# Merge inputs loaded tile by tile with the mLSTM product first, and an attention iteration of four positions, in a fused encoder layer on one core

## The chip, the cores and the metric

The kernel runs on one core of a Trainium2 chip. The metric is the device time of one execution in microseconds (us), and three executions of each kernel are given as a median with the lowest and the highest. The engines are named as in the profile: PE is TensorE (matrix products; PEld its weight loads), DVE is VectorE, ACT is ScalarE, POOL is GpSimd, and SP is the engine from whose queue nearly all DMAs are issued.

## The reference

One encoder layer over two sequences, a prompt of 1024 tokens and a sample of 2048 tokens, of width 1024, each with 16 learned meta tokens put in front. Cut to what matters here:

```python
xn = rmsnorm(h, g_pre)
proj = xn @ w_in + b_in                          # 1024 -> 6672 columns
na_q, na_k, na_v, na_z, ml_qk, ml_v, ml_z, ml_o, ml_g, mg = split(proj)
ya = (neighbourhood_attention(na_q, na_k, na_v, na_rpb) * silu(na_z)) @ w_a    # 512 -> 1024
yb = (mlstm(conv(ml_qk), ml_v, ml_g, ml_o, head_g)   * silu(ml_z)) @ w_b       # 512 -> 1024
ga, gb = split(sigmoid(mg))
y  = (ga * ya + gb * yb) @ w_out                 # the merge, 1024 -> 1024
out = h + rmsnorm(y, g_post)                     # meta tokens dropped
```

The attention has 8 heads of 64 and sees windows of 8 grid rows by 16 columns with a relative bias `na_rpb`. The mLSTM has 4 heads of 128 and runs in both directions. All products are carried to nearly float32 precision.

## The kernel before, in words

**Products.** Every float32 operand is split into a high part in the PE's format (an ACT copy, `AF.Copy`) and the remainder (a DVE subtraction), and a product is three matmuls: high by high, high by low, low by high (`mm3`, lines 144 to 146).

**Two streams on PE.** The order of PE's instructions is written out by the program; the other engines' orders come from the compiler's scheduler. Two Python generators make the order. `dense` yields, after each handful of matmuls, what they cost PE: mostly `6 * C512` (six matmuls of 512 columns, 1.41 us) or `12 * C256` (1.44 us). `sparse` runs the mLSTM and the attention, whose steps depend on ACT and DVE, and yields after each step how much dense work should follow it. `run` adds up what `sparse` yields, and draws dense pieces until that is used up; when `dense` yields `True` it cannot go on, and `sparse` continues alone.

**The dense stream** follows `PLAN`: the input projection in groups of columns (`m` for the mLSTM, `n` for the attention, `g` for the merge gates) for sequence 0 (the prompt) and for the two halves of sequence 1 (the sample), and merges `("f", s, b)`, one for each 512 tokens. The plan is m and n of sequence 0, m of both halves of sequence 1, n of its second half, g of sequence 0, merges (0,0) and (0,1), then n and g of what is left, and merges (1,0) to (1,3), which are the end of the kernel.

**The sparse stream** follows `STEPS`: mLSTM of sequence 0, attention of sequence 0 (row tiles 0 and 1), mLSTM of sequence 1, attention of sequence 1 (row tiles 0 to 3). An mLSTM starts with its gates (`ml_gates`: a load of `g_t`, then `yield 3.0`, then small steps, the first PE step being line 754 and the next line 762), goes on with states and outputs, and ends with a normalisation (`ml_norm`, whose transposes are line 1205).

**The attention** (`na`) takes a row tile of 512 tokens, a pair of heads (`pr`, 0 to 3), a head (`hh`) and a column block (`cb`, 0 to 3): 64 units for sequence 0 and 128 for sequence 1. An iteration has three positions, each ended by `yield A_NA` with `A_NA` = 1.52: the scores of unit u (lines 665 and 666), then the scaling of u and the turning of u-1 (transposes, line 690), then the output product of u-2 (line 702). The steps of `na_prep`, which load and split the inputs of the next head, are spread over the positions. Ahead of the first unit the prep runs with `5 + 5 * 1` yields of `A_NA`. After the last column block of a head pair, line 710 multiplies by the gate and line 711 stores the pair's tile to `YA`; when `pr` is 3 the row tile is entered in `self.done`.

**The merge** (`final`) of a tile needs eight tiles of 128 by 512: four of `YA[s][b]` (k = 0 to 3, attention, one for each pair of heads) and four of `YB[s]` (k = 4 to 7, mLSTM). `yload` loads them into `yr` tiles (the ring `st` of 4 buffers, shared with the projection's stores and the residual loads `xres`) and splits them (lines 1248 and 1249). It returns at once unless all eight are done (`ready`). Otherwise it is spread beside the work before the merge, as a hook in the second half of the previous merge or as the side of a projection group; if it was not, `final` runs all of it at its start. The first half of a merge, called F1 here, goes over eight feature tiles `ft`: for `br` = 0 (attention) and then 1 (mLSTM) a product over four k into a PSUM bank, a gated multiply (line 1284, whose gate tiles `tg` are loaded two feature tiles ahead into the ring `stT`), and after the second the sum and its split `mh`, `mlo`. Beside F1 runs `final_out` of the previous merge: residual loads `xres`, line 1377, stores. The second half, F2, is `w_out`: lines 1305 to 1307, with `yo` out of it. Weights come through `whi` and `wlo`, rings of 4 buffers, 512 KB for each load, in the order of use, on SP like all else. SP issues in order: a DMA that waits holds those behind it.

Of the kernel before, what the change touches and what calls it, by code (L numbers as in the profile page):

```python
# [17 lines left out]
P = 128  # L18
# [86 lines left out]

NBW = 4
C512, C256 = 0.235, 0.12
A_NA, A_D, A_A, A_N, A_G = 1.52, 1.63, 1.63, 1.85, 1.3


class K:
# [384 lines left out]
    def spread(self, gen, chunks, until=None):  # L496

        steps = 22 if until is None else 12

        def side(last=False):  # L500
            nonlocal acc, over
            acc += steps / chunks
            while not over and (acc >= 1.0 or last):
                acc -= 1.0
                x = next(gen, "end")
                over = x == "end" or (until is not None and x == until)
        acc, over = 0.0, False
        return side

    def group(self, s, t0, meta, cols, reuse, nxt):  # L510

        todo = [(s, t0, meta), (s, t0 + 512, False)]
        jobs = self.layout(cols)
        nb = None
        for j, (kind, c) in enumerate(jobs):
            if kind == "tm":
                yield from self.tm_unit(c[0], [(x,) + h for x, h in zip(self.xs, todo)], c[1])
                continue
            ws = self.wtake(len(c))
            last = j == len(jobs) - 1  # L520
            for hf in range(2):
                side = None
                if j == 0 and hf == 0 and not reuse:
                    side = self.spread(self.build_half(*todo[1], self.xs), 15)
                elif last and nxt and nxt[0] == "f":
                    side = self.spread(self.yload(*nxt[1:]), 15) if hf else None
                elif last and nxt:
                    if hf == 0:
                        nres = []
                        nb = self.build_half(*nxt, nres)  # L530
                        side = self.spread(nb, 15, "scaled")
                    else:
                        side = self.spread(nb, 15)
                for col, w in zip(c, ws):
                    for cost in self.fm_half(col, w, self.xs[hf], *todo[hf], done=self.wdone if hf else None):
                        yield cost
                        if side:
                            side()
# [13 lines left out]
    def na(self, s, rts):  # L552

        tc, nc, i = self.tc, self.nc, self.i
        rows = _row_types(SEQLEN[s] // 64)
        with tc.tile_pool(name=f"na{s}{rts[0]}", bufs=1, side="right", reuse_waits="tile") as np_:
            self.qB = [np_.tile([P, 4, P], F32R, name=f"qB{j}") for j in range(2)]
            self.kx = [np_.tile([P, 16, 64], F32R, name=f"kx{j}") for j in range(2)]
            self.gts = [np_.tile([P, 17, 48], F32, name=f"gt{j}") for j in range(2)]
            for q in self.qB:  # L560
                nc.gpsimd.dma_start(q[64:128], i["onehot"].rearrange("a (b c) -> a b c", b=4))
            for g in self.gts:
                nc.gpsimd.memset(g[:, 0, :], 0.0)
                nc.gpsimd.memset(g[:, 16, :], 0.0)
            heads = [(rt, pr, hh) for rt in rts for pr in range(4) for hh in range(2)]
            n = len(heads)
            prep = self.na_prep(np_, s, rows, heads, 0)
            for k in range(6):
                next(prep, None)
                for _ in range(1 if k else 5):  # L570
                    yield A_NA
            self.na_bias(rows, heads, 0)
            cur, nxt = self.head, None
            units = [(j, cb) for j in range(n) for cb in range(4)]
            ready = {}
            for u in range(len(units) + 2):
                if u < len(units):
                    j, cb = units[u]
                    if cb == 0:
                        cur = self.head  # L580
                        prep = self.na_prep(np_, s, rows, heads, j + 1) if j + 1 < n else iter(())
                        next(prep, None)
                    ready[u] = [cur, heads[j], cb, None, None, self.gts[j % 2]]
                    self.na_scores(np_, ready[u], rows)
                    if j + 1 < n and cb == 0:
                        self.na_bias(rows, heads, j + 1)
                yield A_NA
                if u < len(units):
                    self.na_scale(np_, ready[u])
                    if cb:  # L590
                        next(prep, None)
                if 1 <= u <= len(units):
                    self.na_turn(np_, ready[u - 1], rows)
                yield A_NA
                if u >= 2:
                    self.na_out(np_, ready.pop(u - 2), s)
                if u < len(units) and cb >= 2:
                    next(prep, None)
                yield A_NA

    def na_bias(self, rows, heads, j):
# [94 lines left out]
    def na_out(self, np_, unit, s):  # L696
# [12 lines left out]
        if hh and cb == 3:  # L709
            nc.vector.tensor_tensor(yg, yg, zt, op=ALU.mult)  # L710
            nc.sync.dma_start(self.YA[s][rt][pr][:, :], yg)
            if pr == 3:
                self.done.add(("na", s, rt))


    def ml_gates(self, s, keep, mp, res):
# [9 lines left out]
            nc.gpsimd.memset(gt[:, 0, 8 * d + 4:8 * d + 8], 1.0e4)  # L726
        nc.sync.dma_start(gt[:NM, 0, :], self.GA[s][0:NM, :])
        nc.sync.dma_start(gt[:, 1:, :], self.GA[s][NM:, :].rearrange("(c p) g -> p c g", p=P))
        yield 3.0
        gv = gt.rearrange("p c (d k h) -> p d k c h", d=2, k=2)  # L730
        lf = t("g_lf", [P, 2, NC_, 4])
        e = t("g_e", [P, 2, NC_, 4])
# [495 lines left out]
        self.done.add(("ml", s))  # L1228


    def ready(self, s, b):
        return {("ml", s), ("na", s, b)} <= self.done

    def yload(self, s, b):

        if not self.ready(s, b):
            return
        nc, fp, n = self.nc, self.wp, 512
        yh = fp.tile([P, KT, n], F32R, name="yh", tag="xh", bufs=2)
        yl = fp.tile([P, KT, n], F32R, name="yl", tag="xl", bufs=2)  # L1240
        self.y = (s, b), yh, yl
        yr = {}
        for k in range(KT + 2):
            if k < KT:
                yr[k] = fp.tile([P, n], F32, name="yr", tag="st", bufs=4)
                nc.sync.dma_start(yr[k], self.YA[s][b][k][:, :] if k < 4 else self.YB[s][k - 4][:, b * n:(b + 1) * n])
            if k >= 2:
                nc.scalar.activation(yh[:, k - 2], yr[k - 2], AF.Copy)  # L1248
                nc.vector.tensor_tensor(yl[:, k - 2], yr.pop(k - 2), yh[:, k - 2].bitcast(F32), op=ALU.subtract)  # L1249
                yield  # L1250

    def final(self, s, b, nxt):
        nc, fp, i = self.nc, self.wp, self.i
        n, t0 = 512, 512 * b
        if self.y is None or self.y[0] != (s, b):
            for _ in self.yload(s, b):
                pass
        _, yh, yl = self.y
        mh = fp.tile([P, KT, n], F32R, name="mh", tag="xh", bufs=2)
        ml = fp.tile([P, KT, n], F32R, name="mlo", tag="xl", bufs=2)  # L1260
# [2 lines left out]
        def gates(ft):  # L1263
            if ft < KT:
                tgs[ft] = []
                for br in range(2):
                    tg = fp.tile([P, n], F32, name="tg", tag="stT", bufs=4)
                    nc.sync.dma_start(tg, self.GT[s][8 * br + ft][:, t0:t0 + n])
                    tgs[ft].append(tg)

        gates(0)
        gates(1)
        for ft in range(KT):
            w = self.wtake(1)[0]
            ms = tgs.pop(ft)
            for br in range(2):
# [5 lines left out]
                if br:  # L1282
                    self.wdone()
                nc.vector.scalar_tensor_tensor(ms[br], ms[br], 1.0, p, op0=ALU.add, op1=ALU.mult)
                if br:
# [23 lines left out]
        for cq in range(4):  # L1309
# [7 lines left out]
            for tt in range(4):  # L1317
# [19 lines left out]
                if nxt and hook is None:  # L1337
                    if nxt[0] != "f":
                        nres = []
                        hook = self.build_half(*nxt, nres)  # L1340
                    elif self.ready(*nxt[1:]):
                        hook = self.yload(*nxt[1:])
                if hook:
                    next(hook, None)
                yield (3 if tt in first else 12) * C256
        if hook:
            for _ in hook:
                pass
        if nxt:
            self.fout = self.final_out(s, t0, yt, ssq, 0, 4)  # L1350
            if nxt[0] != "f":
# [31 lines left out]
    def dense(self, ctx):  # L1383
# [19 lines left out]
        for j, (s, t0, cols) in enumerate(PLAN):  # L1403
            nxt = PLAN[j + 1] if j + 1 < len(PLAN) else None
            if s == "f":
                if post is None:
                    post = self.gpost = self.gain("g_post")
                while not self.ready(t0, cols):
                    yield True
                yield from self.final(t0, cols, nxt and (nxt if nxt[0] == "f" else nxt[:2] + (False,)))  # L1410
                continue
            same = [0 <= k < len(PLAN) and PLAN[k][:2] == (s, t0) for k in (j - 1, j + 1)]
# [81 lines left out]
```

## Time and profile before

| | |
|---|---|
| time, three runs | 2925.31 us median (2923.33 to 2926.53) |
| the profiled execution | 2927.06 us, its span 2925.1 us |
| PE busy | 2824.3 us, 97% |
| DVE, ACT busy | 1745.3 us (60%), 1287.4 us (44%) |
| granted PE clock, mean over the span | 0.986 |
| DMA | 675.26 MB, mean 231 GB/s |

The span is what the profiler's records cover; the time of the execution is 1.96 us longer. A busy PE is not a PE at its peak, since the profile models the ends of matmuls, so the distance between the starts of matmuls is read beside it. Idle time of an engine other than PE costs nothing by itself.

### The profile page before, as it was taken

To read this page: it belongs to the slowest core of one execution; us is meant where nothing else is said; L and a number is where in the kernel's file an instruction comes from. 1 tells how busy PE (TensorE), PEld (TensorE's weight loads), DVE (VectorE), ACT (ScalarE), POOL (GpSimd) and SP (SyncE) were. 2 spreads that over 40 slices of the span, in tenths; PEclk is the share of its full clock that TensorE was granted. 3 is DMA by queue.
4 is the path that set the end of the run, shared out by engine and by line. 5 is a ranking of instruction groups with operands and counts; after the bars stand their busy time and mean duration, and the time that the engine had idled before them with its cause. 6 is when DMAs were issued, how large, how long until landed. Compare 5 with 4: busy or idle time off the path is not lost.

```text
span 2925.1 us, 49552 instructions
## 1 busy us (share of the span) xinstructions
PE 2824.3 (97%) x17488; PEld 2514.2 (86%) x17488; DVE 1745.3 (60%) x4722; ACT 1287.4 (44%) x3114; POOL 23.0 (1%) x107
## 2 busy tenths in 40 slices
PE   6999999999799999899999999999999999999998
PEld 6998898899689988798887998888888888979877
DVE  5233566556556765466558786565555557786843
ACT  4112546443344444356566554523444445544421
POOL 1000000000000000000000000000000000000000
PEclk9999999999899999999999999999999999999999
DMA  9655566755775654469669898578569659797875
GB/s 348 222 174 184 194 224 235 251 180 195 254 248 155 200 167 142 138 219 312 212 213 356 279 346 281 154 261 273 178 190 298 192 163 289 249 303 242 274 245 194
DMA packets 438760, 675.26 MB, mean 231 GB/s; under 512 B 52240, under 2 KB 253024, under 8 KB 438512
## 3 DMA queue, kind: packets, MB, share of 16 engines
q1 hardware_dynamic: 437392, 669.41, 70.0%
q0 software_dynamic: 1120, 2.69, 0.4%
q8 instruction: 138, 2.26, 0.3%
q14 instruction: 110, 0.90, 0.1%
HBM read 455.05 MB, written 216.90 MB: 230 GB/s over the span
## 4 chain that ended last, share of the span: by engine, by line
PE 82%; DMA 9%; DVE 5%; ACT 1%; SPq 1%; issue 1%; ACTq 0%; DVEq 0%
PE pj L144 14%; PE pj L145 14%; PE pj L146 14%; PE pj L412 6%; PE pj L413 6%; PE pj L414 6%; PE pj L1305 3%; PE pj L1307 3%; PE pj L1306 3%; PE sm L702 3%; PE tr L690 3%; DMA tg<-gt 1%; PE sc L665 1%; PE sc L666 1%; PE sm L146 1%; DMA um<-ud 1%
## 5 line engine op out<-in xcount | busy, mean ns | idle before, releaser
L144 PE MATMUL pj<-xh,whi 128*128 128x512 f32 (+1 forms) x1824 | 722.3, 396 | 1.0 <-DVE xl L310 1.0
L145 PE MATMUL pj<-xl,whi 128*128 128x512 f32 (+1 forms) x1824 | 702.3, 385 | 0.1
L146 PE MATMUL pj<-xh,wlo 128*128 128x512 f32 (+1 forms) x1824 | 700.5, 384 | 0.0
L412 PE MATMUL pj<-whi,xh 128*128 128x256 f32 (+3 forms) x1576 | 451.0, 286 | 0.0
L413 PE MATMUL pj<-wlo,xh 128*128 128x256 f32 (+3 forms) x1576 | 444.6, 282 | 0.0
L414 PE MATMUL pj<-whi,xl 128*128 128x256 f32 (+3 forms) x1576 | 444.1, 282 | 0.0
L146 PEld LDWEIGHTS pj<-xh,wlo 128*128 128x128 f32 x1824 | 345.5, 189 | 72.3
L144 PEld LDWEIGHTS pj<-xh,whi 128*128 128x128 f32 x1824 | 346.0, 190 | 55.9 <-DVE xl L310 1.2
L145 PEld LDWEIGHTS pj<-xl,whi 128*128 128x128 f32 x1824 | 346.5, 190 | 53.2 <-DVE xl L310 0.4
L412 PEld LDWEIGHTS pj<-whi,xh 128*128 128x128 f32 (+1 forms) x1576 | 294.3, 187 | 1.2
L413 PEld LDWEIGHTS pj<-wlo,xh 128*128 128x128 f32 (+1 forms) x1576 | 294.0, 187 | 1.0
L414 PEld LDWEIGHTS pj<-whi,xl 128*128 128x128 f32 (+1 forms) x1576 | 293.9, 187 | 0.9
L673 ACT ACTIVATE prb<-sc,mx 128x384 f32<-128x384 f32 (+2 forms) x192 | 120.1, 625 | 237.4 <-DVE mx L669 236.3
L1305 PE MATMUL pj<-whi,mh 128*128 128x256 f32 x768 | 221.7, 289 | 2.7 <-DVE yo L1333 2.7
L1307 PE MATMUL pj<-whi,mlo 128*128 128x256 f32 x768 | 217.7, 283 | 0.0
L1306 PE MATMUL pj<-wlo,mh 128*128 128x256 f32 x768 | 217.4, 283 | 0.0
L669 DVE CUSTOM_DVE_ANT_1 sc<-sc,gt 128x384 f32<-128x384 f32 (+2 forms) x192 | 118.9, 619 | 96.3 <-PE sc L666 86.8
L708 DVE TENSOR_TENSOR yg<-sm,yg 64x128 f32<-64x128 f32 x384 | 108.4, 282 | 108.0 <-ACT yg L706 100.2
L421 DVE TENSOR_TENSOR stT<-pj,bb 128x256 f32<-128x256 f32 (+3 forms) x197 | 83.2, 422 | 143.8 <-PE pj L414 142.7
L144 PE MATMUL pj<-yh,whi 128*128 128x512 f32 x384 | 158.3, 412 | 8.5 <-ACT yh L1248 6.1
L693 DVE TENSOR_TENSOR pts<-tr,pts 96x512 fp32r<-96x512 f32 (+2 forms) x192 | 131.6, 685 | 47.8 <-ACT pts L692 46.0
L145 PE MATMUL pj<-yl,whi 128*128 128x512 f32 x384 | 153.9, 401 | 0.2 <-DVE yl L1249 0.2
(234 smaller groups left out, 5074.6 us busy)
## 6 DMA issues: line engine op xcount, KB each, us to landing
whi<-wh SPq DMA_DIRECT2D x176, 512.0 KB
wlo<-wl SPq DMA_DIRECT2D x176, 512.0 KB
wh<-whi SPq DMA_DIRECT2D x64, 512.0 KB
wl<-wlo SPq DMA_DIRECT2D x64, 512.0 KB
wraw<-w_in SPq DMA_DIRECT2D x48, 512.0 KB
gt<-st SPq DMA_DIRECT2D x96, 256.0 KB
tg<-gt SPq DMA_DIRECT2D x96, 256.0 KB
xh<-xh SPq DMA_DIRECT2D x6, 2048.0 KB
```

Of the source, the lines that this page charges most:

```text
L144: mm(out, ah, bh, start=start, stop=False)
L145: mm(out, ah, bl, start=False, stop=False)
L146: mm(out, al, bh, start=False, stop=stop)
L412: nc.tensor.matmul(o, xh, wh, start=k == 0, stop=False)
L413: nc.tensor.matmul(o, xh, wl, start=False, stop=False)
L414: nc.tensor.matmul(o, xl, wh, start=False, stop=k == KT - 1)
L669: nc.vector.tensor_tensor_reduce(out=so, in0=so, in1=gt[:, g0:g0 + ns, c0:c0 + 32], op0=ALU.add, op1=ALU.min, scale=-1.0, scalar=3.0e38, a ...
L673: nc.scalar.activation(pr_[:, :N].rearrange("p (b a c) -> p b a c", b=4, c=8), sc[:, :N].rearrange("p (a b c) -> p b a c", b=4, c=8), AF.E ...
L693: nc.vector.tensor_tensor(pts[:ks, :, 1, :], pt[:ks], pts[:ks, :, 0, :].bitcast(F32), op=ALU.subtract)
L1305: nc.tensor.matmul(o, mh[:, k, xs], wh, start=k == 0, stop=False)
L1306: nc.tensor.matmul(o, mh[:, k, xs], wl, start=False, stop=False)
L1307: nc.tensor.matmul(o, ml[:, k, xs], wh, start=False, stop=k == KT - 1)
```

## The change

Three things are changed.

1. **Merge inputs.** The attention's stores are entered in `self.done` for each pair, `("na", s, b, pr)`, instead of for the row tile. `yload` takes the mLSTM's tiles first, then the attention's pairs; where a tile is not yet done it splits what it holds and yields `"wait"`, on which the loops beside it leave off. It is started always (`ystart`), also when its inputs are not all done. `final` does the mLSTM product (`br` = 1) ahead of the attention product (`br` = 0), and takes each tile when its product needs it; where that is not to be had it yields `True`, in place of the loop ahead of the merge that waited for `ready`.
2. **Attention iteration.** Four positions with `A_NA` = 1.12 instead of three with 1.52: scores of u; scaling of u; turning of u-1; output of u-2. The prep ahead of the first unit has `6 + 5 * 2` yields.
3. **mLSTM gates.** The yield after the load of `g_t` is 6.0 instead of 3.0.

The core of the diff:

```diff
-A_NA, A_D, A_A, A_N, A_G = 1.52, 1.63, 1.63, 1.85, 1.3
+A_NA, A_D, A_A, A_N, A_G = 1.12, 1.63, 1.63, 1.85, 1.3
...
-                for _ in range(1 if k else 5):
+                for _ in range(2 if k else 6):
                     yield A_NA
...
                     self.na_scale(np_, ready[u])
                     if cb:
                         next(prep, None)
+                yield A_NA
                 if 1 <= u <= len(units):
                     self.na_turn(np_, ready[u - 1], rows)
+                    if u < len(units) and cb >= 2:
+                        next(prep, None)
                 yield A_NA
                 if u >= 2:
                     self.na_out(np_, ready.pop(u - 2), s)
-                if u < len(units) and cb >= 2:
-                    next(prep, None)
                 yield A_NA
...
             nc.sync.dma_start(self.YA[s][rt][pr][:, :], yg)
-            if pr == 3:
-                self.done.add(("na", s, rt))
+            self.done.add(("na", s, rt, pr))
...
-        yield 3.0
+        yield 6.0
...
     def yload(self, s, b):
-        if not self.ready(s, b):
-            return
...
+        for k in (4, 5, 6, 7, 0, 1, 2, 3):
+            need = ("ml", s) if k > 3 else ("na", s, b, k)
+            if need not in self.done:
+                while todo:
+                    split()
+                    yield
+                while need not in self.done:
+                    yield "wait"
+            yr = fp.tile([P, n], F32, name="yr", tag="st", bufs=4)
+            nc.sync.dma_start(yr, self.YA[s][b][k][:, :] if k < 4 else self.YB[s][k - 4][:, b * n:(b + 1) * n])
+            todo.append((k, yr))
+            if len(todo) == 3:
+                split()
                 yield
+        while todo:
+            split()
+            yield
...
     def final(self, s, b, nxt):
         if self.y is None or self.y[0] != (s, b):
-            for _ in self.yload(s, b):
-                pass
+            self.ystart(s, b)
+            next(self.ygen)
...
-            for br in range(2):
+            for br in (1, 0):
+                for k in range(4 * br, 4 * br + 4):
+                    while k not in self.yk:
+                        if next(self.ygen) == "wait":
+                            yield True
...
-                    elif self.ready(*nxt[1:]):
-                        hook = self.yload(*nxt[1:])
+                    else:
+                        hook = self.ystart(*nxt[1:])
...
-                while not self.ready(t0, cols):
-                    yield True
```

More of the change, by code (lines that the diff above doesn't have):

```diff
@@ L506, in side @@
                 over = x == "end" or (until is not None and x == until)
+                if x == "wait":
+                    break
         acc, over = 0.0, False
@@ L525, in group @@
                 elif last and nxt and nxt[0] == "f":
-                    side = self.spread(self.yload(*nxt[1:]), 15) if hf else None
+                    side = self.spread(self.ystart(*nxt[1:]), 15) if hf else None
                 elif last and nxt:
@@ L1228, in ml_norm @@
         self.done.add(("ml", s))
-    def ready(self, s, b):
-        return {("ml", s), ("na", s, b)} <= self.done
     def yload(self, s, b):
-        if not self.ready(s, b):
-            return
         nc, fp, n = self.nc, self.wp, 512
@@ L1240, in yload, with split, ystart @@
         yl = fp.tile([P, KT, n], F32R, name="yl", tag="xl", bufs=2)
[L1241 to L1249, printed above, removed]
-                yield
+        self.y, self.yk = ((s, b), yh, yl), set()
+        todo = deque()
+        def split():
+            k, yr = todo.popleft()
+            nc.scalar.activation(yh[:, k], yr, AF.Copy)
+            nc.vector.tensor_tensor(yl[:, k], yr, yh[:, k].bitcast(F32), op=ALU.subtract)
+            self.yk.add(k)
+        for k in (4, 5, 6, 7, 0, 1, 2, 3):
[11 more added lines that the diff above has]
+                split()
+                yield
+        while todo:
+            split()
+            yield
+    def ystart(self, s, b):
+        self.ygen = self.yload(s, b)
+        return self.ygen
     def final(self, s, b, nxt):
@@ L1265, in gates @@
                 tgs[ft] = []
-                for br in range(2):
+                for br in (1, 0):
                     tg = fp.tile([P, n], F32, name="tg", tag="stT", bufs=4)
                     nc.sync.dma_start(tg, self.GT[s][8 * br + ft][:, t0:t0 + n])
-                    tgs[ft].append(tg)
+                    tgs[ft].insert(0, tg)
         gates(0)
@@ L1275, in final @@
             ms = tgs.pop(ft)
-            for br in range(2):
+            for br in (1, 0):
+                for k in range(4 * br, 4 * br + 4):
+                    while k not in self.yk:
+                        if next(self.ygen) == "wait":
+                            yield True
                 p = self.psum("pj", [P, 512])
@@ L1281, in final @@
                         yield 6 * C512
-                if br:
+                if not br:
                     self.wdone()
                 nc.vector.scalar_tensor_tensor(ms[br], ms[br], 1.0, p, op0=ALU.add, op1=ALU.mult)
-                if br:
+                if not br:
                     nc.vector.tensor_tensor(ms[0], ms[0], ms[1], op=ALU.add)
@@ L1346, in final @@
         if hook:
-            for _ in hook:
-                pass
+            for x in hook:
+                if x == "wait":
+                    break
         if nxt:
```

## The prediction

> **What bounds the kernel now.** I read the page's first two parts, then PE's waits, then busy time by stretches where those waits lie, then the chain of waits there, and last the written order of both programs (which instruction stands behind which; it has no times).
>
> ```profile
> PE 2824.3 (97%) x17488; PEld 2514.2 (86%) x17488; DVE 1745.3 (60%) x4722; ACT 1287.4 (44%) x3114; POOL 23.0 (1%) x107
> PE   6999999999799999899999999999999999999998
> PEclk9999999999899999999999999999999999999999
> ```
>
> PE is the bound nearly everywhere. The change adds and removes no matmul, so all it can move is the 101 us in which PE is idle (2925.1 - 2824.3) and the time lost to a lower granted clock after an idle stretch. About 29 us lie ahead of the first matmuls and stay. What the rest waits for:
>
> ```profile
> PE sc L665 <- ACT kd L645: 10.6, 1, 10.6
> PE tr L690 <- DVE prb L682: 9.8, 3, 6.4
> PE pj L144 <- ACT yh L1248: 6.1, 3, 4.4
> PE sm L754 <- issue: 4.9, 1, 4.9
> ```
>
> Columns: us in total, times, longest. In order: the first scores of the prompt's attention; three turnings late in the sample's attention; the start of a merge; the first product of the sample's mLSTM gates. By stretches (length, then busy us of PE, PEld, DVE, ACT, POOL, then granted clock, DMA share, GB/s):
>
> ```profile
> 785.00:800.00 15.00, 4.09 (x16) 2.72 (x15) 1.94 (x3) 2.79 (x4) 0.00 (x0) 0.78 0.80 228
> 1205.00:1215.00 10.00, 10.00 (x40) 7.01 (x39) 2.17 (x14) 1.38 (x5) 0.00 (x0) 0.76 0.43 131
> 2350.00:2400.00 50.00, 50.00 (x252) 41.51 (x251) 28.65 (x69) 23.93 (x49) 0.00 (x0) 1.00 0.60 189
> 2810.00:2820.00 10.00, 4.93 (x20) 3.02 (x19) 4.35 (x17) 1.73 (x4) 0.00 (x0) 0.87 0.95 316
> 2820.00:2830.00 10.00, 8.71 (x24) 6.15 (x25) 6.01 (x9) 1.89 (x3) 0.00 (x0) 0.62 0.71 233
> 2830.00:2850.00 20.00, 20.00 (x89) 16.36 (x88) 11.77 (x18) 2.53 (x4) 0.00 (x0) 1.00 1.00 356
> 2850.00:2860.00 10.00, 7.86 (x28) 5.97 (x27) 4.52 (x7) 0.63 (x1) 0.00 (x0) 0.83 0.99 367
> ```
>
> The third row is attention in full swing: PE never idle. The last four are the last merge, (1,3): its inputs come late, the clock falls, and then DMA is full. The chain (start, us):
>
> ```profile
> 781.84 13.67 DMA mk<-st
> ...
> 801.05 9.30 DMA mk<-st
> 810.36 5.29 DMA kr<-nkm
> ...
> 2806.80 1.99 DMA ya<-yg
> 2808.81 3.59 DMA yr<-ya
> ...
> 2815.01 7.87 DMA yr<-yb
> ...
> 2846.07 7.34 DMA tg<-gt
> ```
>
> The last attention pair is stored at 2806.80 and loaded back at 2808.81, and only behind that, on SP, come the four mLSTM tiles, ready since long.
>
> **The change, part by part** (sum against the profiled execution, 2927.06 us = span 2925.1 + 1.96; it lies 1.75 above the median of 2925.31).
>
> *Merge (1,3).* In the new order its four mLSTM tiles and three of its attention tiles are issued ahead of the last store; only k = 3 follows it. Between the last output product and the first F1 matmul PE now has 8.6 us of F2 matmuls instead of 5.8 (the attention ends earlier), and 12 mLSTM matmuls (12 x 0.232 = 2.8 us) and nine of k = 0 to 2 before k = 3 is needed. Before, PE waited 4.4 us for that tile; it now has 5.6 us more cover, so the tile is there, and nothing waits for k = 4 to 7. PE's side of the gain: idle 5.07 + 1.29 in 2810 to 2830, and busy time at the lower clock, 4.93 x 0.13 + 8.71 x 0.38 = 3.95; together 10.3. Further on the gate load `tg` (2846.07) made PE idle for 2.14 at a clock of 0.83 (7.86 x 0.17 = 1.34): 3.5 more if that goes too, 13.8 in all. What is late next is DMA: from 2810 to the landing of that `tg` at 2853.4 it moved 3.16 + 2.33 + 7.12 + 1.25 = 13.9 MB (the rows' GB/s by their lengths). The four tiles taken out are 4 x 0.262 = 1.05 MB, and the remaining 12.8 MB take 36.0 us at the 356 GB/s of the row from 2830, so the same gate tile comes at 2846.0: 7.4 us earlier, and PE, which could gain 10.3, waits there. I take **-7.4**; the ends are -2.9 (only the 1.05 MB saved) and -13.8.
>
> *Loads put earlier.* Seven loads go into the stretch before, four of them beside the last attention heads around 2720, where a stretch from 2700 to 2720 shows a DMA share of 1.02 at 335 GB/s: 1.05 MB / 335 = 3.1 us if on the path, nothing if F2 (share 0.43 from 2770 to 2800) takes them. **+1.0** (0 to 3.1).
>
> *Attention iteration.* Dense work for a unit goes from 3 x 1.52 = 4.56 to 4 x 1.12 = 4.48. Where PE is never idle that buys and costs nothing: dense pieces cover it. From scores to turning PE time rises from a median 7.4 to 8.4 us; from turning to output it stays at 7.3 (fewest 7.2 before, 5.8 now, against ACT 0.60 + DVE 0.69 to cover). Each of the three waits of line 690 loses about 1 us: **-2.5** (0 to -6, if the lower clock behind them goes too).
>
> *First scores of the prompt.* 16 x 1.12 = 17.9 us of prep yields instead of 15.2. But SP's order changes more: the head's loads (two `qr`, four `kr`) stood behind the second `mk` store, whose product ends 14.0 us of PE time before the scores; now they stand behind the next two weight pairs, two more `mk` stores and an `mq` store, whose product ends 2.8 us before. That store waits for its ACT evacuation, the loads for it, ACT's `kd` for them, PE for `kd`. Low: evacuation 0.68, store issue 0.32, six issues at medians 0.587, 0.546, 0.587 twice each (3.4), landing 5.29, `kd` 0.84: 10.5 - 2.8 = 7.7 idle against 10.6. High: 17.0 us, as from 781.84 to the end of `kd` at 798.8, + 0.68 - 2.8 = 14.9. I take the middle, **+0.7**, since the two weight loads that held up SP before now lie further ahead.
>
> *mLSTM gates.* 3.0 more in the yield puts 2.7 us more matmuls ahead of line 754, which was 4.9 late: -2.7, and of the time lost at the clock of 0.76 (10 x 0.24 = 2.4) I count half: **-3.9** (-1 to -5.1). ACT's logarithm now stands behind a fresh evacuation, which holds the rest. The shift also leaves no dense piece between some gate steps: in the prompt line 762 directly follows 754, in the sample 771 follows 762. The like case is line 822, 0.5 us behind one DVE copy: 2 x 0.5 + 0.5 = **+1.5** (0 to 3). The prompt's gates had no wait to win.
>
> *Merges (0,0) and (0,1).* Every weight is split here for the first time, PE is idle 3.1 of 1545 to 1600 and 3.5 of 1600 to 1650 (DMA share 1.03, DVE 48.3 of 55), and the same operations stand in another order: **0** (-4 to +4). Merges (1,0) to (1,2) had their inputs in time; reading the mLSTM first moves nothing there.
>
> Sum: -7.4 + 1.0 - 2.5 + 0.7 - 3.9 + 1.5 = -10.6, so 2916.5 profiled and **2914.7** as a median.
>
> [...] The trace has full-rate clock again some microseconds after each wait, and 0.83 also behind the wait of 2.1 us at 2851. [...]
>
> **Rivals.**
>
> *DMA does not bind the last merge.* A stretch from 800 to 810 moved 389 GB/s, more than 356, and the `tg` wait may be SP's order rather than bytes. Then the merge gives 13.8: -17.0, **2908.3**. Against it: share 0.99 to 1.00 from 2830 on. [...]
>
> *DMA takes it back.* If `tg` comes only 2.9 us earlier because the residual loads and stores now crowd in, PE sits there longer and the clock falls once more (half of 3.4 us, 1.7; -2.9 + 1.7 = -1.2): -10.6 + 7.4 - 1.2 = -4.4, **2920.9**. For it: the full share; and SP stands still from 2798.5 to 2806.8 at the last store in either version.
>
> *The prompt's first loads are parked too late.* Place: the SP queue behind the `mq` store. If they land as in the chain of before, one behind the other (13.67 + 9.30 + 5.29, with 0.68 and 0.84 around them: 29.8 us), PE is idle 29.8 - 2.8 = 27.0 instead of 10.6, and with 1.6 for the clock the term is +18 instead of +0.7: +6.7, **2932.0**, slower. It decides from a chain of about 29 us on. Against it: 14.0 + 10.6 = 24.6 us is the longest that chain was from product to scores, with an 8 us backlog on SP in it.
>
> *The waiting does nothing.* In the new order no merge starts before its last attention product, so the `"wait"` path leaves nothing undone on PE; all gain is from the order of loads and products. That is already in the sum.
>
> **How the numbers follow.** Forecast 0.48, DMA not binding 0.22, DMA takes it back 0.18, parked loads 0.12. About 0.2% (5.9 us) is what a measurement can tell. Faster: 0.44 of the forecast, 0.22, and 0.03 of the third; slower: 0.12 and 0.02 for the order of merges (0,0) and (0,1) going badly; same: the rest. The range reaches from -22 (DMA not binding, gates and turnings at their good ends) to +4 short of the last rival: 2903 to 2929.
>
> **What would show it.** Right: PE busy throughout 2800 to 2835; line 144's wait for `yh` gone; the wait at the first gates product about 2; one `yr` load after the last `ya` store; a wait on `tg` in the last merge. Wrong: the scores' wait for `kd` or `stk` above 15; idle PE around 1550 to 1650 or 2700 to 2760 by more than now; the stretch from the last attention product (2799.7) to the end of the span, 125.4 us now and 125.4 + 2.8 - 7.4 = 120.8 if the term holds, not below 125.

## The result and the profile after

The changed kernel takes 2914.47 us (median of 20 runs, 2907.72 to 2923.43), the kernel before 2924.62 (20 runs, 2916.56 to 2929.83): ratio 0.9969, 95% interval 0.9961 to 0.9978, some 9 us faster (the medians alone differ by 10.2). The forecast was 2914.7. Its sum came out right; most of its terms did not.

One warning ahead of the profile. Runs of one kernel lie up to 16 us apart, and the profiled execution of the changed kernel took 2923.43 us, the longest of its 20. The two profiled executions differ by 3.6 us only, where the medians differ by 10. So times are compared over all runs, and a profile, which is one execution, serves to say where PE waits. PE is busy for 2818.3 us (96%), before for 2824.3. PE's waits (us in total, times, longest):

```profile
PE sc L668 <- ACT kd L648: 13.1, 1, 13.1
PE tr L693 <- DVE prb L685: 11.5, 5, 7.1
PE pj L144 <- DVE tg L1305: 9.3, 7, 3.0
PE sc L668 <- ACT prb L676: 6.6, 4, 4.6
...
PE sm L756 <- issue: 4.5, 1, 4.5
```

The `yh` wait is gone. The prompt's first scores wait 13.1 instead of 10.6, the turnings 11.5 instead of 9.8, the gates' first product 4.5 instead of 4.9. The waits for the gate tiles `tg` of merges have grown from 2.4 to 9.3, those of scores for `prb` from 3.1 to 6.6. By stretches, columns as before:

```profile
785.00:800.00 15.00, 6.17 (x27) 4.65 (x25) 0.69 (x1) 0.69 (x1) 0.00 (x0) 0.86 0.97 342
...
2810.00:2820.00 10.00, 10.00 (x74) 9.42 (x73) 3.71 (x14) 2.06 (x7) 0.00 (x0) 1.00 0.75 242
2820.00:2830.00 10.00, 10.00 (x45) 8.18 (x44) 7.84 (x16) 1.16 (x2) 0.00 (x0) 1.00 0.98 334
2830.00:2850.00 20.00, 17.60 (x76) 13.64 (x74) 8.88 (x13) 1.37 (x3) 0.00 (x0) 1.00 1.00 382
2850.00:2860.00 10.00, 9.03 (x33) 7.34 (x34) 5.31 (x8) 1.26 (x2) 0.00 (x0) 0.83 0.91 339
```

The first row is the prompt's first scores: DVE and ACT have next to nothing to do, DMA is full, and PE waits for the head's loads. The last merge runs at full clock from 2810 to 2830, where before PE was busy 4.93 and 8.71 of 10 at 0.87 and 0.62. It then waits for a gate tile, as the chain of waits shows (start, us):

```profile
2835.22 7.21 DMA tg<-gt
...
2843.15 6.98 DMA tg<-gt
```

**Lost time.** To compare versions I add up, for one profiled execution, how much longer the distances between the starts of matmuls are than those of the same matmuls where nothing holds them (0.232 us with 512 columns, 0.12 with 256, 0.11 below). It holds waits and low clock alike, and little else differs between versions: the profiled time less this sum is the same within 1.0 us in all fourteen executions. Two figures of the written order stand beside it, in us of PE work that the order itself puts there: the **lead**, from the last attention product to the first matmul of the last merge, and the **cover**, from the end of the product whose store stands just ahead of the prompt's first head loads on SP to the first scores.

| kernel | lead | cover (store) | 700–860 | 1160–1290 | 2500–2800 | from 2800 | ratio |
|---|---|---|---|---|---|---|---|
| before | 5.8 | 13.9 (`mk`) | 30.0 | 14.0 | 24.5 | 15.2 | 1 |
| after | 8.6 | 2.8 (`mq`) | 28.4 | 10.1 | 28.2 | 5.5 | 0.9969 |
| e1_merge | 5.8 | 13.9 (`mk`) | 27.1 | 12.7 | 30.2 | 2.7 | 0.9992 |
| e2_four | 15.7 | 16.7 (`mk`) | 23.6 | 17.7 | 17.6 | 6.1 | 0.9952 |
| e3_gates | 0.1 | 0.0 (`mq`) | 26.9 | 12.2 | 28.1 | 17.5 | 1.0027 |
| e4_attfirst | 8.6 | 2.8 (`mq`) | 25.5 | 10.7 | 28.8 | 6.9 | 0.9964 |
| e5_nores | 8.6 | 2.8 (`mq`) | 26.4 | 9.6 | 23.5 | 6.5 | 0.9962 |
| e6_pool | 8.6 | on POOL | 21.4 | 9.1 | 22.9 | 4.1 | 0.9979 |
| e7_fourmerge | 15.7 | 16.7 (`mk`) | 20.8 | 20.0 | 15.3 | 2.4 | 0.9945 |
| e8_lead3 | 15.7 | 16.7 (`mk`) | 22.0 | 17.7 | 19.1 | 7.6 | 0.9959 |
| e9_lead | 21.4 | 13.9 (`mk`) | 25.2 | 9.7 | 20.1 | 5.0 | 0.9945 |
| e10_prep7 | 0.1 | 16.7 (`mk`) | 20.8 | 15.0 | 21.3 | 19.0 | 0.9990 |
| e11_gprompt | 12.9 | 2.8 (`mq`) | 27.1 | 13.4 | 20.3 | 4.5 | 0.9992 |
| e12_gsample | 12.9 | 16.7 (`mk`) | 20.0 | 13.0 | 26.8 | 3.7 | 0.9962 |

The stretches (us from the span's start) are: the prompt's first scores; the sample's gates; merges beside the last attention heads; the last merge and the end. In e10_prep7 a wait of 10.4 us begins at 2800.0, inside the last merge, and is counted to it. Each row is one execution, and by how much a stretch changes from one execution of a kernel to the next was not measured.

### The profile page after: what moved, and what is told of

The parts are those of the page before. It is cut to its first block, busy times and chain, and to the rows that moved or that the text cites. A ratio compares the mean times of both kernels' runs of the same rounds, so it can differ in the third digit from the quotient of the medians.

```text
span 2921.6 us, 49506 instructions
## 1 busy us (share of the span) xinstructions
PE 2818.3 (96%) x17488; PEld 2511.0 (86%) x17488; DVE 1742.9 (60%) x4722; ACT 1289.8 (44%) x3114; POOL 23.2 (1%) x107
## 4 chain that ended last, share of the span: by engine, by line
PE 80%; DMA 9%; DVE 7%; issue 2%; ACT 1%; SPq 1%; DVEq 0%; ACTq 0%
PE pj L144 13%; PE pj L145 13%; PE pj L146 13%; PE pj L412 6%; PE pj L413 6%; PE pj L414 6%; PE pj L1326 3%; PE pj L1328 3%; PE pj L1327 3%; PE sm L705 3%; PE tr L693 2%; DMA tg<-gt 2%; DMA um<-ud 1%; PE sc L668 1%; PE sc L669 1%
## 5 line engine op out<-in xcount | busy, mean ns | idle before, releaser
L695 ACT ACTIVATE pts<-tr 96x512 fp32r<-96x512 f32 (+2 forms) x192 | 114.1, 594 | 115.9 <-PE tr L693 115.6
```

## The experiments

Each ratio is over all runs, against the kernel before on the same chip; it can differ by 0.0004 from that of the medians. Three groups of four kernels shared their chips; the medians of before were 2922.78, 2918.39 and 2918.97 us.

### First group: each part alone, and the order of the products

**e1_merge**: the changed kernel with the attention iteration and the gates put back, so that only the merge part is left.

```diff
-A_NA, A_D, A_A, A_N, A_G = 1.12, 1.63, 1.63, 1.85, 1.3
+A_NA, A_D, A_A, A_N, A_G = 1.52, 1.63, 1.63, 1.85, 1.3
...
-                for _ in range(2 if k else 6):
+                for _ in range(1 if k else 5):
...
-        yield 6.0
+        yield 3.0
```

> The merge part alone, on the kernel before. By the sum of the prediction: -7.4 + 1.0 = -6.4 us against before. Rival (all of the gain is the last merge, in which the profile after lost 5.7 us to waits and a low clock instead of 15.4, and the other two edits only deal the remaining waits out anew): -9 to -11 us, as much as the whole change. In the profile, by either: the wait for yh at the last merge gone, PE busy from 2800 to 2835.

Measured: 2920.93 us (12 runs), ratio 0.9992 [0.9980, 1.0005], -2 us and not to be told from nothing. In its profile the last merge has won nearly all it could: lost time from 2800 on is 2.7 instead of 15.2. The stretch ahead of it lost 5.7 more (30.2 instead of 24.5); the waits of scores for `prb` are 8.4 in all instead of 3.1. But the two profiled executions differ by 10.8 us (2916.30 against 2927.06) where the medians differ by 2. So the gain in the last merge is there in this execution, and why the runs as a whole show so little of it, the profile does not tell.

**e2_four**: the kernel before with the attention iteration of the change alone.

```diff
-A_NA, A_D, A_A, A_N, A_G = 1.52, 1.63, 1.63, 1.85, 1.3
+A_NA, A_D, A_A, A_N, A_G = 1.12, 1.63, 1.63, 1.85, 1.3
...
-                for _ in range(1 if k else 5):
+                for _ in range(2 if k else 6):
...
+                yield A_NA
                 if 1 <= u <= len(units):
                     self.na_turn(np_, ready[u - 1], rows)
```

> The four positions alone (with A_NA 1.12 and the longer prep), on the kernel before. By the sum: -2.5 + 0.7 = -1.8 us, line 690's wait shorter by about 1 us each. Rival (waits dealt out anew): 0 within 4 us, with line 690's wait not shorter, since it ends on a DMA that comes late however long PE has other work. In both the last merge keeps its wait for yh of 4 us and its low clock.

Measured: 2908.84 us (6 runs), ratio 0.9952 [0.9937, 0.9967]: -14 us, more than the whole change. This was not foreseen by any of the theories.

**e3_gates**: the kernel before with the longer yield of the gates alone.

```diff
-        yield 3.0
+        yield 6.0
```

> The gates' yield of 6.0 alone, on the kernel before. By the sum: -3.9 + 1.5 = -2.4 us, the wait at the first product of the sample's gates 2.2 us instead of 4.9. Rival: about 0, the wait stays near 4.5 as in the profile after, because ACT's logarithm stands behind a fresh evacuation or the load of g_t comes later too.

Measured: 2931.74 us (11 runs), ratio 1.0027 [1.0016, 1.0039]: **slower** by 8 us. Its PE waits:

```profile
PE sc L665 <- ACT kd L645: 14.8, 1, 14.8
PE pj L144 <- ACT yh L1248: 9.5, 1, 9.5
...
PE sm L754 <- issue: 4.9, 1, 4.9
```

The wait that the yield is put against stays at 4.9. Two others grow: `kd` from 10.6 (the prompt's head loads now stand behind the `mq` store) and the last merge's `yh` from 4.4 (the attention ends just ahead of the merge, lead 0.1).

**e4_attfirst**: the whole change, but with the attention's tiles and product first in the merge.

```diff
-        for k in (4, 5, 6, 7, 0, 1, 2, 3):
+        for k in range(8):
...
-            for br in (1, 0):
+            for br in (0, 1):
```

> The whole change, but with the attention product and the attention tiles first again; the loading tile by tile is kept. If reading the mLSTM product first matters, the last merge waits for its fourth attention tile: by the chain 8.6 us of matmuls and 2.1 of the first three tiles now cover it, 2.8 less than in the changed kernel, so a wait of 0 to 2 us there and a time 0 to +4 us against the changed kernel, the mLSTM tiles being loaded in time or up to 2 us late behind the last store. Rival (loading early is all that counts): no difference beyond 2 us and no wait for yh.

Measured: 2913.23 us (12 runs), ratio 0.9964 [0.9952, 0.9975], the changed kernel's within the intervals. A `yh` wait of 3.0 is back, and the longest `tg` wait is 1.1 instead of 3.0. The `yh` wait is not for the fourth attention tile but for the last mLSTM tile: in this order the four mLSTM tiles are again issued behind the last attention store, from 2804.95 to 2808.73. So this run does not load them early. Taking the mLSTM first does what the prediction said of it, but it is worth only 1.4 us of lost time here (5.5 from 2800 on instead of 6.9), which the times cannot show.

The three parts alone give -2, -14 and +8, in sum -8 against -9 for all: roughly additive, though nothing like the terms of the prediction.

### Second group: what the last merge waits for, and why the iteration gains

**e5_nores**: the changed kernel without the residual loads of merge (1,2), which run beside the last merge: 2 MB less. That merge's output adds its own value in place of the residual.

```diff
-            if j < len(todo):
+            if j < len(todo) and (s, t0) != (1, 1024):
```

> The whole change, with the 2 MB of residual loads of merge (1,2), which run beside the first half of the last merge, left out (that merge adds its own value in place of the residual). If DMA's bytes bind the last merge (the prediction's term: 12.8 MB at 356 GB/s), 2 MB less are 5.6 us of DMA, so the wait for tg in the last merge (3.0 in the profile after, the clock at 0.83 behind it) goes, and the time falls by 3 to 5 us against the changed kernel. If it is SP's order or nothing in particular that makes the tile late, the wait stays near 3 and the time within 2 us.

Measured: 2907.72 us (5 runs), ratio 0.9962 [0.9950, 0.9975], not to be told from the changed kernel's 0.9969; with these intervals a gain of 3 us cannot be excluded by the time. Its stretches and its wait:

```profile
2820.00:2840.00 20.00, 16.45 (x61) 12.94 (x60) 6.73 (x11) 1.26 (x2) 0.00 (x0) 0.83 0.83 286
2840.00:2860.00 20.00, 20.00 (x106) 17.10 (x105) 9.42 (x14) 2.53 (x4) 0.00 (x0) 1.00 0.79 269
```

```profile
PE pj L144 <- DVE tg L1305: 8.9, 6, 3.5
```

DMA has room now (shares, the last column but one, of 0.83 and 0.79), and the longest wait for `tg` is still 3.5. On SP, eight output stores stand in a row from 2811 to 2819, and the next gate loads are issued behind them at 2820. So full DMA was not what made the gate tile late, or not alone; that the queue's order did it is read from the trace. Since the stores moved as well, this run does not measure what the bytes cost by themselves.

**e6_pool**: the changed kernel, the first head's loads of each attention issued by POOL.

```diff
-            self.nc.sync.dma_start(
+            eng.dma_start(
...
+        eng = nc.gpsimd if j == 0 else nc.sync
```

> The whole change, but the loads of the first head of each sequence are issued by POOL instead of SP, so that they no longer stand behind the mq store. If standing there is what makes the prompt's first scores late (13.1 us of waiting in the profile after, the store's product ending only 2.8 us of PE time before them), the wait falls by 6 to 13 us and the time by 6 to 13 against the changed kernel. If the loads are late for DMA's own load there (share 0.97 from 785 to 800), the wait stays above 9 and the time within 3 us.

Measured: 2913.49 us (9 runs), ratio 0.9979 [0.9966, 0.9991].

```profile
PE sc L669 <- DVE stk L647: 6.4, 1, 6.4
```

The first scores wait 6.4 instead of 13.1, and the stretch 700 to 860 loses 21.4 instead of 28.4. That is the place on SP shown as the cause of that wait. Yet the median is not better than the changed kernel's, so 7 us won in one stretch were not kept; where they went this run does not tell, since its one profiled execution (2906.42) was much shorter than its median.

**e7_fourmerge**: the changed kernel with the gates' yield back at 3.0 (and so e1's and e2's parts together).

```diff
-        yield 6.0
+        yield 3.0
```

> The whole change without the gates' 6.0. In the order, the last attention product then stands 15.7 us of PE time before the last merge (8.6 with all, 5.8 before, 15.7 with four positions alone), and the first loads of the prompt's attention behind the second mk store with 16.7 us of cover (2.8 with all). Theory now: what counts is how far the attention's end leads the last merge and what the first loads stand behind; the gates' edit spoils both. Then 2907 to 2910, as with four positions alone, since the merge part has nothing left to win there. The prediction's sum would have it 2.4 us slower than the whole change, 2917.

Measured: **2902.67 us** (5 runs, 2901.39 to 2905.18), ratio 0.9945 [0.9933, 0.9958]. This version beats both kernels: 16 us under the kernel before, and about 7 under the changed one (0.9969 - 0.9945 = 0.24%). Two PE waits of it:

```profile
PE sm L756 <- DVE g_lf L750: 8.4, 1, 8.4
...
PE sc L668 <- ACT kd L648: 6.5, 1, 6.5
```

The gates' wait is 8.4, nearly twice the 4.5 of the changed kernel, `kd` is down to 6.5, and the last merge loses 2.4.

**e8_lead3**: the kernel before with three positions, the same amount of dense work for a unit as with four, and 7 + 5 yields ahead.

```diff
-A_NA, A_D, A_A, A_N, A_G = 1.52, 1.63, 1.63, 1.85, 1.3
+A_NA, A_D, A_A, A_N, A_G = 4.48 / 3, 1.63, 1.63, 1.85, 1.3
...
-                for _ in range(1 if k else 5):
+                for _ in range(1 if k else 7):
```

> The kernel before, with three positions and the same dense work for a unit as four positions have (A_NA 4.48/3) and as much prep ahead of the first unit (12 yields, 17.9 us). In the order it has the same lead of 15.7 us and the same cover of 16.7 us as four positions alone. If lead and cover are the cause, it is as fast as four positions alone: 2909 within 3 us. If the fourth position is (more time from scores to turning), it stays near the kernel before, 2921 to 2924, with lines 690 waiting about 10 us.

Measured: 2906.85 us (5 runs), ratio 0.9959 [0.9945, 0.9972], the gain of e2_four within the intervals. The fourth position is not what gains. The amounts are.

### Third group: which amount it is

**e9_lead**: only the first of e8's two edits.

```diff
-A_NA, A_D, A_A, A_N, A_G = 1.52, 1.63, 1.63, 1.85, 1.3
+A_NA, A_D, A_A, A_N, A_G = 4.48 / 3, 1.63, 1.63, 1.85, 1.3
```

> The kernel before with A_NA = 4.48/3 in place of 1.52 and nothing else. In the written order the last merge then follows the last attention product by 21.4 us of other matmuls instead of 5.8; the prompt's first head loads stand where they stood, with the same 13.9 us of cover ahead of the first scores. Theory (the attention's end against the last merge is what counts): -10 to -13 against the kernel before, ratio 0.9955 to 0.9965, the loss of the last merge (14.8 of the profile of before) down to 3 to 7. Rival 1 (the yields ahead of the prompt's first unit made the gain of the earlier version with 7 + 5 of them): 0 to -3. Rival 2 (a shift of this kind only reshuffles where loss falls): within 3 us either way.

Measured: 2903.69 us (6 runs), ratio 0.9945 [0.9931, 0.9960]. One constant, 1.52 to 1.493, gains 15 us, a little more than was expected, and level with the best version. The prompt's `kd` wait, at its old place and cover, is 9.5 instead of 10.6; little was won there. The last merge loses 5.0, in the range given, and the stretch ahead of it 20.1 instead of 24.5.

**e10_prep7**: only the second.

```diff
-                for _ in range(1 if k else 5):
+                for _ in range(1 if k else 7):
```

> The kernel before with 7 + 5 instead of 5 + 5 yields of A_NA ahead of the prompt's first unit and nothing else: cover of the first scores 16.7 instead of 13.9, and only 0.1 us instead of 5.8 between the last attention product and the last merge in the written order. Theory (the attention's end counts): the wait for kd falls from 10.6 to about 7.8 (-3), and the last merge loses up to 5.7 more and a low-clock stretch: 0 to +5 in sum, ratio 1.000 to 1.002. Rival (the yields ahead of the first unit are the gain): -8 to -12.

Measured: 2916.57 us (12 runs), ratio 0.9990 [0.9977, 1.0002]. Of its waits:

```profile
PE pj L144 <- ACT yh L1248: 10.4, 2, 10.2
...
PE sc L665 <- ACT kd L645: 6.3, 1, 6.3
```

The yields ahead of the first unit shorten the `kd` wait by 4.3 and, at a lead of 0.1, `yh` of the last merge is waited for 10.2 instead of 4.4. As waits the two nearly cancel. The rival that gave the whole gain to these yields falls.

**e11_gprompt** and **e12_gsample**: the changed kernel with 6.0 for one sequence and 3.0 for the other.

```diff
-        yield 6.0
+        yield 3.0 if s else 6.0
```

(e12_gsample: `6.0 if s else 3.0`.)

> The changed kernel with the gates' yield of 6.0 for the prompt alone, 3.0 for the sample. The last merge is 12.9 us behind the last attention product; the prompt's first head loads stand behind the mq store (2.8 us of cover), as in the changed kernel. Theory (both the place of the loads and the lead count, some 3 us each): ratio 0.996, between the changed kernel (0.9969) and the one with 3.0 in both (0.9945); the wait for kd at 12 to 14, the last merge's loss at 2 to 5. Rival (only the lead counts): 0.9945 to 0.995.

> The changed kernel with the gates' yield of 6.0 for the sample alone, 3.0 for the prompt. The last merge is again 12.9 us behind the last attention product, but the prompt's first head loads stand behind the second mk store (16.7 us of cover). Theory: the wait for kd about 7, and the wait at the sample's first gates product, 8.4 with 3.0, down to about 4.5: ratio 0.993 to 0.9945, the fastest of all; about 3 to 6 us below the version with 6.0 for the prompt alone, which is then the price of the parked loads. Rival (the place of the loads costs nothing): the two alike within 2 us.

Measured: 2916.73 us (12 runs), ratio 0.9992 [0.9981, 1.0004], with 6.0 for the prompt; 2907.93 (6 runs), ratio 0.9962 [0.9947, 0.9977], with 6.0 for the sample. Both gain less than the theory said, e11 less than the rival too, and e12 is not the fastest. Their difference, 8.8 us, is more than the 3 to 6 expected: at the same lead, the prompt's longer yield is the bad one. In the profile the prompt's first scores have 12.1 of wait against 6.5 and 27.1 of lost time against 20.0; from 2500 to 2800 it is the other way round (20.3 against 26.8), so one execution of each does not account for the 8.8. The sample's longer yield does what it was meant to: 5.7 of wait at line 756 instead of the 7.8 of e11 and the 8.4 of e7.

## Why the prediction was right, and where it was not

The sum of -10.6 stood against some -9 measured, but most of its terms do not stand. By its steps:

**Last merge, -7.4.** Right in kind, some 2 us too small in the profile: 15.2 - 5.5 = 9.7 of lost time went. The signs named ahead came: PE busy throughout 2800 to 2835, no `yh` wait, a single `yr` load behind the last `ya` store, a wait on `tg`. The figure for the end of the span had a wrong start: the last attention product starts at 2804.6 and not at 2799.7, which is the one before it. From there to the end it is 120.5 us before and 113.5 after (from 2808.1), so -7.0 instead of the -4.6 forecast, with the 2.8 us of longer lead included. One reading was wrong: of the 4.4 us of wait before, taken for the last attention tile, none was for it. That tile (k = 3) was waited for 0.4 us; the 4.4 were for the first mLSTM tile, as ACT's copy shows:

```profile
2818.32 0.63 ACT L1248 ACTIVATE yh<-yr 128x512 fp32r<-128x512 f32 x1 [5.27 <-DMA yr<-yb]
```

So in the last merge it is taking the four mLSTM tiles out from behind the last store that gains. That DMA binds there was the reason given for the size; the share was 1.00 at 382 GB/s, but e5_nores took bytes away and the wait stayed. The changed kernel reached 406 from 2848 to 2852, so the row of 356 was no limit; what set the tile's time is not separated. What failed in the larger picture is that the term was taken to reach the end time undiminished: alone, this part gains 2 us (e1_merge), though the profile of that version shows 12.5 us less lost from 2800 on.

**Attention iteration, -2.5.** The step failed, twice. The size: alone it gives -14. The cause: the term was put on the turnings, by the PE time from scores to turning. Those waits did not shrink (9.8 to 11.5), and the trace shows why distance does not matter to them. The longest one of the changed kernel, in order of time:

```profile
2592.72 0.75 DVE L1399 SCALAR_TENSOR_TENSOR yo<-yo,nwy,xres 128x512 f32<-128x512 f32 x1 [6.83 <-DMA xres<-x_sample]
...
2597.52 0.47 DVE L685 TENSOR_SCALAR prb<-prb,sm 128x512 f32<-128x512 f32 x1
...
2598.13 1.09 PE L693 MATMUL tr<-ident,prb 128*128 128x128 f32 x4 [7.06 <-DVE prb L685]
```

DVE stood 6.83 us at the residual add of another merge (line 1377 before, 1399 after), whose load had not landed, and the turning's input was queued behind it. Before it is the same, by DVE's waits:

```profile
DVE yo L1377 <- DMA xres<-x_sample: 12.0, 8, 4.6
```

This is read in the traces; no run took those loads away.

The gain of the iteration comes from an amount that the prediction wrote down and set at nothing: dense work of 4.48 instead of 4.56 a unit. Over 192 units of attention that is 192 x 0.08 = 15 us, by which the attention runs ahead of the dense stream. "Where PE is never idle that buys and costs nothing" holds at the place, but not at the end: with a lead of 15.7 or more the last merge's inputs are stored that much earlier, and in e2, e8 and e9 its wait for `yh` is gone without any change to the merge. Without the fourth position (e8_lead3), and by the constant alone (e9_lead), the gain is the same within the intervals. That the amount makes the gain is shown; how is shown in part only, since e1_merge won as much in the last merge and 2 us in all. The prediction saw the lead of 8.6 in the whole change, and used it in the merge only.

**First scores of the prompt, +0.7.** Measured +2.5 in the wait (13.1), between the ends given; the lost time of the whole stretch fell by 1.6 in the profile (30.0 to 28.4). But the term mixed two things that the runs hold apart. The place behind the `mq` store comes from the gates' yield: with it back at the `mk` store the wait is 6.3 to 7.4, so the place costs some 6; and the yields ahead win 3 to 4 (10.6 to 6.3 in e10). The bounds were sound: 2.8 of cover + 13.1 = 15.9 us from product to scores, within the 10.5 to 17.7. At the `mk` store the sum of cover and wait is 23 to 24.5 in every version, so there each us of cover is a us less of wait.

**Gates, -3.9 and +1.5.** This step failed in sign: +8 alone and about +7 inside the change (e7 against after). The wait at line 754 fell by 0.4, not by 2.7. With the old yield it would have been 8.4 in the new iteration (e7), so there the yield wins some 4; on the old iteration it wins nothing (4.9 in e3). What raises the wait to 8.4 are the yields ahead of the first unit: it is 7.4 in e10, which changes them alone, and 3.9 in e9, which leaves them. The term of +1.5 for missing dense pieces shows as one wait of 0.4, at line 764. What the yield costs lies elsewhere, in what it moves past other work: the prompt's head loads on SP (some 6), and the lead (15.7 to 8.6). That these two make up the +8 is not shown: in e3 the stretch of the first scores lost 3.1 less than before, though its wait for `kd` grew by 4.2. A remaining wait of about 2 us did not come about; behind the 4.5 the granted clock was 0.83 from 1205 to 1215, where before it was 0.76.

**Merges (0,0) and (0,1), 0**, and **loads put earlier, +1.0**. In the changed kernel's execution the stretch 1540 to 1760 lost 17.9 instead of 10.8; in the other versions with the new merge it is 9.8 to 15.1. From 2700 to 2800, where the loads put earlier were expected to cost, 0.3 more was lost in the changed kernel and 2.0 more in e1, within the 0 to 3.1. But the prediction also said that nothing moves in merges (1,0) to (1,2), and there the traces show a price that it left out, near 2510, beside the second half of merge (1,0). Of the changed kernel:

```profile
2508.86 5.27 DMA yr<-ya
2514.15 0.63 ACT yh L1243
2514.78 0.68 ACT prb L676 x2
```

ACT stands at the copy of an input of merge (1,1) until its load has landed, and the scores' `prb` is queued behind it, as on DVE above. PE waits 4.6 us there, and a stretch at half clock follows (0.50 from 2516.2 to 2519.6), which costs 1.7. In the five versions with the new merge and a lead of up to 8.6 this wait is 3.0 to 4.8; before it is 1.0, and with the new merge and a lead of 12.9 or more at most 0.3. In e1 it makes up 3.8 of the 5.7 that the stretch from 2500 to 2800 lost more, and the half clock 1.7. This is read in the traces too; no run moved that load.

So parts measured at -14 and +8 came to -6, where the prediction had -2.5 + 0.7 - 3.9 + 1.5 = -4.2 for them, and the merge came to -2 instead of -6.4: two large errors cancelled, and the total is right by luck. Of the rivals, the parked loads have the right place, but PE waits 13.1 and not 27.0 there: +2.5 against before, some 6 against the `mk` place, and not +18. That DMA takes the last merge's gain back is not borne out (9.7 less was lost); that DMA does not bind it agrees with e5, but the gain was not 13.8, since a wait for `tg` stayed.

**What stays open.** By lead, lost time from 2500 on goes from 40 to 46 (lead 0.1) over 33 to 40 (5.8) and 27 to 36 (8.6) to 18 to 31 (12.9 and more). Its part from 2800 on follows the inputs of the last merge: 15.2 to 19.0 where PE waits 4 to 10 us for `yh` (before, e3, e10), 2.4 to 7.6 elsewhere. From 2500 to 2800 the executions with a lead of 15.7 or 21.4 lose 15 to 20, those below 20 to 30. The wait on ACT near 2510 is a part of that, and the rest is open; the waits on `xres` of 4.6 and 6.8 that are 1.5 to 2.5 in the versions with 15.7 are a candidate, against which e9 with 4.4 and e3 with 1.9 speak. Nor is it clear why e11, with more lead than the changed kernel, is slower by 0.23%, or where e6's 7 us went.

## What to carry to other kernels

Where two streams are woven by amounts of work, the sum of the amounts places the ends of the streams against each other, and that can be worth more than any local fit: write down, from the order alone, how far apart the producer's end and the consumer's start lie, and do it for every edit, the small constants above all. An amount added ahead of one step moves everything behind it past loads in the DMA queue; ask which store the next loads will stand behind, and how far ahead of their use its product ends. When a wait names an engine, look at what that engine itself was held by: the cause can be the load of quite another stage, as where DVE stood 6.83 us at the residual add of another merge.

## What the runs showed of the hardware

A lower granted clock stands behind some of PE's waits and not behind others. In the changed kernel it was 0.84 from 757 to 768, with a wait of 2.5 us in it, and 0.83 from 812 to 822, with one of 2.6; from 2721 to 2735, with one of 3.0, it was 1.00. So in these three it is not the length of the wait alone that decides, and what does was not measured.

What such a stretch costs can be read: in the kernel before PE waited 2.1 us between 2852 and 2855, and the granted clock was 0.50 from 2855.0 to 2858.3 with PE busy throughout, so some 1.7 us came on top of the wait.

Runs of one kernel spread by more than many of the effects here: the kernel before by 13 and 17 us on two chips (13 and 23 runs). The two fastest versions lie within 4 and 7 us, but over 5 and 6 runs only, so that their spread is smaller is not shown.
